# Twelve modulation units: where they run, and five of them on TensorE strips

## The chip, the cores and the metric

The kernel runs on one core of a Trainium2 chip, in float32, with the large products split into float32r pieces. The metric is the device time of one execution in microseconds (us). Several executions are timed, and their median counts. A profile, taken of one execution, shows what the engines did: PE is TensorE (PEld its weight loads), DVE is VectorE, ACT is ScalarE, POOL is GpSimd, SP is SyncE, whose queue issues nearly all transfers.

## The reference, cut to what matters

Two transformer blocks run one after the other on 256 tokens of width 2048. The first is an RWKV7 mixer and a convolutional FFN, each with a modulated norm before it and a gated norm behind it. The modulation is a vector of six segments of 2048 numbers, and its product with a matrix of 2048 x 12288 (100 MB) is what the change is about:

```python
mod = jax.nn.silu(c) @ ada_w + ada_b
sh_m, sc_m, g_m, sh_f, sc_f, g_f = jnp.split((mod + ada_table[layer])[:, None, :], N_MOD, axis=-1)
h = _rms(x, norm_mix_pre[layer]) * (1 + sc_m) + sh_m
y, v_first = _rwkv7_mix(h, ...)          # r, k, v, w, a, g projections, scan over time, @ w_o
x = x + g_m * _rms(y, norm_mix_post[layer])
h = _rms(x, norm_ffn_pre[layer]) * (1 + sc_f) + sh_f
f = _conv_ffn(h, ...)
x = x + g_f * _rms(f, norm_ffn_post[layer])
```

Segments 0 and 1 (sh_m, sc_m) are needed at once. Segment 2 (g_m) is needed when the output projection of the mixer is scaled, segments 3 and 4 (sh_f, sc_f) when the FFN's input is made, segment 5 (g_f) at the FFN's end. The second block (attention, short convolution, gate) takes no part in the change.

## The kernel before

**Stages.** On the profile's clock: a v and k stage to about 300 us; an r stage to about 503 us, a loop over 16 pairs of heads, j, with the projection of r and what the scan needs of each pair; the scan, with a head of its own to about 585 us and then four chunks of 64 tokens to about 745 us; the output projection, four column blocks of w_o, to about 863 us; the residual with its norms and the transposition for the FFN (`add_residual`, `to_fm`) to about 890 us; then the FFN and the second block.

**The head of the scan** is a list of names, HEAD, whose entries are issued in that order: `d` the 32 x 32 diagonal products (`diag_gram`, line 655 on TensorE), `v0` the inversion of the diagonal blocks of half 0 on VectorE (lines 659 to 685), `g` the gram products (line 701), `b` the products with the centring matrix (line 715), `i0` the off-diagonal part of the inversion (lines 735 and 743), `e` one of four e_proj units: one load of w_proj, four matmuls (line 871) and two stores (line 874). The chunk loop behind it issues stage_r (line 757), stage_u (line 774) and the state and output products (from line 788) of a chunk, and beside them, step by step, the inversion of half 1, the norm of the chunk before and the late units.

**The order.** The code's order is not the engines' order. A scheduler reorders instructions under the dependences, and buffers and PSUM banks are taken from pools of fixed size. Within an engine the order is then fixed: an instruction that waits holds those behind it. The SP queue, too, works in order, and a load waits there until its buffer is free.

**Modulation units.** A unit is 512 columns of one segment: 16 row blocks of 128 x 512, loaded two at a time (512 KB a load) into buffers "raw". A unit is cut into four steps of two loads. There are two ways to sum it:

- `ada_group` multiplies each row block by its entries of silu(c) and adds it up, elementwise: VectorE does three of four blocks (lines 240 and 246), ScalarE the fourth (lines 238 and 243) with GpSimd adding (line 244). The 128 rows of the sum are added at the unit's end by matmuls with a column of ones (`ada_fm`, line 281, after line 279 has joined the two sums).
- `ada_group_pe` lets TensorE do the products: the row block is the moving operand, and the stationary one is `sil32`, silu(c) padded with zeros to 32 columns. Four such matmuls stand on four strips of 32 columns of the array and write four quarters of the rows of one PSUM bank ("a"). ScalarE copies the bank at the end (line 268), and `ada_fm` closes the unit as before. Segments 0 and 1 are summed so, in the v and k stage (line 264, loads of line 258).

Twelve late units, segment 2 (units 0 to 3), 4 (units 4 to 7) and 3 (units 8 to 11), go by `ada_group`: 48 steps. A step is taken wherever the code says `next(ada)`: 12 in the r stage (all j but those with j % 8 in RSKIP), 26 in the chunk loop (ASTEP), 6 in the output projection (OSTEP), and the last four where `to_fm` needs the segment. The units of segment 5 have an iterator of their own in the FFN. From the scan on the raw buffers are a ring of three (NADA2), which e_proj shares, against five (NADA) in the v and k stage. Of the PSUM banks with tag "m", used for `ada_fm` and for most short products, the flag `wide_m` makes a third one out of bank "a" when that is not used otherwise.

## Time and profile before

| what | value |
| --- | --- |
| runs timed | 2203.95, 2208.15, 2225.73 us, median 2208.15 |
| the profiled execution, its time | 2202.33 us |
| its span, first to last instruction | 2200.5 us |
| mean granted TensorE clock | 0.938 |
| PE busy | 2007.2 us (91%) |
| DVE busy | 1390.0 us (63%) |
| ACT busy | 1025.5 us (47%) |
| POOL busy | 770.4 us (35%) |
| moved by DMA | 445.26 MB, 202 GB/s in the mean |
| ada_w loads | 192 of 512 KB |
| line 246 (DVE products of the units) | 176, 184.5 us |
| line 244 (POOL sums of the units) | 48, 75.5 us |

Busy shares are means over stages that differ; what matters for a change is the stage it stands in, and in that stage the engine or transfer that the others wait for. The granted clock is a share of 2.4 GHz: 1.0 is the upper level, 0.5 the lower one (1.2 GHz), and a value between is a mix of both. A row of a time order gives the start, the duration, the engine, the line, what is written and read, and how many instructions the row sums up; the bracket at its end is the idle time before it and what ended that.

### The profile page before, as it was taken

The numbers are of one execution on the slowest core, as the hardware profiler recorded it, in microseconds if no ns is written. First come the engines' busy times: TensorE is split into PE (matmuls) and PEld (weight loads), VectorE is DVE, ScalarE is ACT, GpSimd is POOL, SyncE is SP. The second block draws the span as 40 slices with busy tenths as digits, with TensorE's granted clock in tenths as the row PEclk, the third lists the DMA queues.
The fourth block names the chain that finished last, engine by engine and source line by source line (L and its number), as shares of the span: only waits on it lengthen the run. The fifth ranks groups of instructions, "written<-read, shape, count | busy, mean of one in ns | idle before, by whom it ended". The sixth has DMA issues, their size and how long they took to land.

```text
span 2200.5 us, 36863 instructions
## 1 busy us (share of the span) xinstructions
PE 2007.2 (91%) x14708; PEld 1752.7 (80%) x14708; DVE 1390.0 (63%) x1975; ACT 1025.5 (47%) x1594; POOL 770.4 (35%) x437
## 2 busy tenths in 40 slices
PE   6889988987799696899999999999998999999998
PEld 3578777876577475789989999878886799998887
DVE  3576998987877767786666675433335565656435
ACT  3434455553344434555545545444435454454443
POOL 2332445656145334343333232222322222222232
PEclk9999998999679698899999999999999999999999
DMA  8778567774566687676676565665554444456554
GB/s 293 252 249 301 180 207 240 241 230 96 140 160 182 224 288 261 219 270 197 197 215 203 193 209 191 196 214 189 188 190 145 147 158 163 160 163 209 186 194 152
DMA packets 189037, 445.26 MB, mean 202 GB/s; under 512 B 40121, under 2 KB 62777, under 8 KB 187329
## 3 DMA queue, kind: packets, MB, share of 16 engines
q1 hardware_dynamic: 188864, 442.91, 62.4%
q8 instruction: 115, 1.88, 0.3%
q14 instruction: 58, 0.47, 0.1%
HBM read 427.10 MB, written 15.75 MB: 201 GB/s over the span
## 4 chain that ended last, share of the span: by engine, by line
PE 51%; DVE 5%; DMA 4%; ACT 1%; issue 1%; POOL 1%; SPq 0%; ACTq 0%; POOLq 0%; DVEq 0%
PE ps_s L158 6%; PE ps_s L160 6%; PE ps_s L159 5%; PE ps_s L175 4%; PE ps_s L174 4%; PE ps_s L173 4%; PE ps_g L158 4%; PE ps_g L160 4%; PE ps_g L159 4%; PE ps_g L173 3%; PE ps_g L175 3%; PE ps_g L174 3%; DMA raw<-in_ada_w 2%; DVE acc L246 1%; DVE wlo L147 1%
## 5 line engine op out<-in xcount | busy, mean ns | idle before, releaser
L143 ACT ACTIVATE whi<-raw 128x1024 fp32r<-128x1024 f32 x558 | 588.5, 1057 | 647.7 <-PE ps_s L174 126.5
L147 POOL TENSOR_TENSOR wlo<-raw,whi 128x1024 fp32r<-128x1024 f32 x185 | 458.1, 2477 | 984.6 <-ACT whi L143 950.0
L147 DVE TENSOR_TENSOR wlo<-raw,whi 128x1024 fp32r<-128x1024 f32 x373 | 480.3, 1290 | 439.5 <-ACT whi L143 435.2
L160 PE MATMUL ps_g<-xh,wlo 128*128 128x256 f32 x816 | 235.5, 289 | 7.6 <-DVE wlo L147 7.0
L160 PE MATMUL ps_s<-xh,wlo 128*128 128x256 f32 x816 | 230.7, 283 | 9.6 <-DVE wlo L147 9.3
L159 PE MATMUL ps_g<-xl,whi 128*128 128x256 f32 x816 | 235.0, 288 | 2.5 <-POOL xl L1022 2.5
L158 PE MATMUL ps_g<-xh,whi 128*128 128x256 f32 x816 | 235.8, 289 | 0.7 <-DVE kac L407 0.6
L158 PE MATMUL ps_s<-xh,whi 128*128 128x256 f32 x816 | 230.1, 282 | 2.6 <-ACT whi L143 2.6
L159 PE MATMUL ps_s<-xl,whi 128*128 128x256 f32 x816 | 229.6, 281 | 0.0
L246 DVE SCALAR_TENSOR_TENSOR acc<-raw,sil,acc 128x512 f32<-128x512 f32 x176 | 184.5, 1048 | 28.0 <-DMA raw<-in_ada_w 26.6
L160 PEld LDWEIGHTS ps_g<-xh,wlo 128*128 128x128 f32 x816 | 160.5, 197 | 10.4 <-DVE wlo L147 9.6
L160 PEld LDWEIGHTS ps_s<-xh,wlo 128*128 128x128 f32 x816 | 156.5, 192 | 11.4 <-DVE wlo L147 10.7
L159 PEld LDWEIGHTS ps_g<-xl,whi 128*128 128x128 f32 x816 | 161.7, 198 | 4.7 <-POOL xl L1022 2.7
L158 PEld LDWEIGHTS ps_g<-xh,whi 128*128 128x128 f32 x816 | 160.9, 197 | 4.4 <-ACT whi L143 1.3
L158 PEld LDWEIGHTS ps_s<-xh,whi 128*128 128x128 f32 x816 | 156.7, 192 | 3.0 <-ACT whi L143 3.0
L159 PEld LDWEIGHTS ps_s<-xl,whi 128*128 128x128 f32 x816 | 157.3, 193 | 0.0
L244 POOL TENSOR_TENSOR acc<-acc,nbr 128x512 f32<-128x512 f32 x48 | 75.5, 1572 | 140.6 <-ACT nbr L243 139.7
L158 PE MATMUL ps_s<-h3h,whi 128*128 128x256 f32 x384 | 109.6, 285 | 0.0
L160 PE MATMUL ps_s<-h3h,wlo 128*128 128x256 f32 x384 | 108.8, 283 | 0.0
L159 PE MATMUL ps_s<-h3l,whi 128*128 128x256 f32 x384 | 108.4, 282 | 0.0
L373 DVE SCALAR_TENSOR_TENSOR mt<-xx,vec,h 128x256 f32<-128x256 f32 x96 | 75.5, 828 | 6.9 <-POOL yl L377 4.7
L158 PEld LDWEIGHTS ps_s<-h3h,whi 128*128 128x128 f32 x384 | 72.5, 189 | 3.6 <-issue 3.5
(519 smaller groups left out, 4981.7 us busy)
## 6 DMA issues: line engine op xcount, KB each, us to landing
raw<-in_w_f SPq DMA_DIRECT2D x258, 512.0 KB, 4.4
raw<-in_ada_w SPq DMA_DIRECT2D x192, 512.0 KB, 5.2
raw<-in_w_i2f SPq DMA_DIRECT2D x80, 512.0 KB, 3.7
raw<-in_w_o SPq DMA_DIRECT2D x60, 512.0 KB, 4.7
raw<-in_w_v SPq DMA_DIRECT2D x32, 512.0 KB, 4.0
raw<-in_w_k SPq DMA_DIRECT2D x32, 512.0 KB, 4.3
raw<-in_w_r SPq DMA_DIRECT2D x32, 512.0 KB, 6.7
raw<-in_w_g SPq DMA_DIRECT2D x32, 512.0 KB, 4.7
```

Source lines behind the costliest of these rows:

```text
L143: S.activation(hi, raw, AF.Copy)
L147: e.tensor_sub(lo, raw, hi)
L158: mm(acc, wh[:, sl], xh[:, kt, :], start=(kt == 0), stop=False)
L159: mm(acc, wh[:, sl], xl[:, kt, :], start=False, stop=False)
L160: mm(acc, wl[:, sl], xh[:, kt, :], start=False, stop=(kt == KT - 1))
L173: mm(a, xh, wh[:, sl], start=st, stop=False)
L174: mm(a, xl, wh[:, sl], start=False, stop=False)
L175: mm(a, xh, wl[:, sl], start=False, stop=sp_)
L244: G.tensor_tensor(acc, acc, tp, op=ALU.add)
L246: V.scalar_tensor_tensor(acc, raw[:, a, :], sc, acc, op0=ALU.mult, op1=ALU.add)
L373: V.scalar_tensor_tensor(mt[:, i, :], xx[:, k0 + i, :], vcol(V_MU, m * 16 + k0 + i), hx[:, k0 + i, :], op0=ALU.mult, op1=ALU.add)
```

## The change

Three things are changed. **Where the steps are taken:** the r stage takes 4 steps (the last four j in the code, RSTEP) instead of 12, which is all of unit 0; the list HEAD gets 20 entries "a" of one step each, which are units 1 to 5; the 24 steps left, units 6 to 11, are taken in the chunk loop, whose table ASTEP is as before; the output projection takes none, and whatever were left is drained before it. **How five units are summed:** ON_PE names the units 1 to 5, which now go by `ada_group_pe`. **What that needs:** the pool that held `sil32` is closed by then, so `pad_sil` makes it again in the scan's pool, by a memset of GpSimd and a copy of VectorE; and `wide_m` is off during the head, since bank "a" is the accumulator there.

```diff
 NADA2 = 3
-HEAD = "d0 e v0 g0 b0 d1 g1 b1 e i0 e".split()
+HEAD = "d0 e v0 a a a g0 a a a b0 a a a d1 a a a g1 a a a b1 a a a e i0 a a e".split()
 ASTEP = (A01, A01, (0, 1, 1, 0, 1, 1, 0, 1, 1, 0, 1, 1), (1, 1, 1, 1, 1, 1, 0, 0))
-OSTEP = (2, 2, 2, 0)
+OSTEP = (0, 0, 0, 0)
 TFP = 8
-RSKIP = (0, 4)
+RSTEP = 4
+
+ON_PE = (1, 2, 3, 4, 5)
...
-                mm(acc[r:r + 32, :w_], sil32[:, b, :], raw[:, a, :], start=(b < 4), stop=(b >= KT - 4))
+                mm(acc[r:r + 32, :w_], sil32[0][:, b, :], raw[:, a, :], start=(b < 4), stop=(b >= KT - 4))
...
-    sil32 = t_(pa, [P, KT, 32], "sil32")
-    G.memset(sil32, 0.0)
-    V.tensor_copy(sil32[:, :, 0], sil)
+    sil32 = [None]
+
+    def pad_sil(pl):
+        sil32[0] = t_(pl, [P, KT, 32], "sil32")
+        G.memset(sil32[0], 0.0)
+        V.tensor_copy(sil32[0][:, :, 0], sil)
+
+    pad_sil(pa)
...
-    ada_how[0] = ada_group
-    ada = ada_run(ADALAG, *[ada_row(2, k0, 4, V_NMP, gmd) for k0 in range(0, KT, 4)],
-                  *[ada_scale(4, k0, 4, D_AF, V_NFP) for k0 in range(0, KT, 4)],
-                  *[ada_shift(3, k0, 4, D_BF) for k0 in range(0, KT, 4)])
+    late = []
+    for u in range(12):
+        ada_how[0] = ada_group_pe if u in ON_PE else ada_group
+        k0 = u % 4 * 4
+        late.append(ada_row(2, k0, 4, V_NMP, gmd) if u < 4 else ada_scale(4, k0, 4, D_AF, V_NFP) if u < 8
+                    else ada_shift(3, k0, 4, D_BF))
+    ada = ada_run(ADALAG, *late)
...
-        if j % 8 not in RSKIP:
+        if j >= NPAIR - RSTEP:
             next(ada, None)
...
     pc_ = phs.enter_context(pool("scan", 1, reuse_waits="tile"))
+    pad_sil(pc_)
+    wide_m[0] = False
...
     for nm in HEAD:
         run(HD[nm]())
     ada_pool[0] = 1
+    wide_m[0] = True
...
+    for _ in ada:
+        pass
     ada_pool[0] = 1
     phb.close()
```

Line numbers of the changed kernel are higher: by 2 up to the stages, by 10 to 15 behind them (655 is 667, 735 is 747, 788 is 800, 264 is 266, 246 is 248, 228 is 230).

On TensorE, ahead of the first state product of chunk 0 (line 788), these rows stand in the kernel before; `TQ` is the inverted diagonal block, `raw` with `ys` an e_proj unit, `uv` and `rs` are operands of the first chunk:

```order
2440 L743 MATMUL ps_m<-xh,TQ 32x32 x32
2441 L871 MATMUL ps_g<-raw,ys 128x512 x3
2442 L757 MATMUL ps_s<-uv,xh 64x64 x8
2443 L735 MATMUL ps_a<-TQ,xl 32x32 x16
2444 L735 MATMUL ps_m<-TQ,xl 32x32 x16
2445 L757 MATMUL ps_s<-uv,xh 64x64 x8
2446 L774 MATMUL ps_s<-rs,xh 64x64 x8
2447 L757 MATMUL ps_s<-uv,xh 64x64
2448 L743 MATMUL ps_m<-xl,TQ 32x32 x16
2449 L743 MATMUL ps_a<-xl,TQ 32x32 x16
2450 L757 MATMUL ps_s<-uv,xh 64x64 x7
2451 L788 MATMUL ps_g<-uv,BK 64x64 x2
```

In the changed kernel the same place, ahead of line 800, reads as follows; `raw` with `sil` are the units (the buffer's name is sil32, its digits are cut off):

```order
2461 L266 MATMUL ps_a<-raw,sil_4959 32x512 x2
2462 L769 MATMUL ps_s<-uv,xh 64x64 x3
2463 L786 MATMUL ps_s<-rs,xh 64x64 x16
2464 L266 MATMUL ps_a<-raw,sil_4959 32x512 x4
2465 L283 MATMUL ps_m<-cst,nbr 128x1 x4
2466 L747 MATMUL ps_m<-TQ,xl 32x32 x16
2467 L266 MATMUL ps_a<-raw,sil_4959 32x512 x8
2468 L883 MATMUL ps_g<-raw,ys 128x512 x4
2469 L266 MATMUL ps_a<-raw,sil_4959 32x512 x8
2470 L883 MATMUL ps_g<-raw,ys 128x512 x4
2471 L747 MATMUL ps_a<-TQ,xl 32x32 x16
2472 L800 MATMUL ps_g<-uv,BK 64x64 x2
```

Between the stage_r and stage_u products and the first state product stand now the end of unit 4, all 16 matmul pairs of unit 5 and two e_proj units.

On the SP queue, the head of the scan begins in the kernel before with these rows (`ed` are stores of e_proj, `gmd` one of a finished segment-2 unit, `bl` and `gl` loads of the first chunk's norm):

```order
190 L694 DMA uv<-vd 64x2048 x2
191 L874 DMA ed<-gl 128x512 x2
192 L826 DMA bl<-bd 128x16x64
193 L228 DMA raw<-in_ada_w 128x2x512
194 L826 DMA bl<-bd 128x16x64
195 L228 DMA raw<-in_ada_w 128x2x512
196 L922 DMA NT<-in_w_o 128x1024
197 L874 DMA ed<-gl 128x512
198 L228 DMA raw<-in_ada_w 128x2x512
199 L874 DMA ed<-gl 128x512
```

and in the changed kernel with these:

```order
190 L706 DMA uv<-vd 64x2048
191 L260 DMA raw<-in_ada_w 128x2x512
192 L886 DMA ed<-gl 128x512
193 L260 DMA raw<-in_ada_w 128x2x512
194 L886 DMA ed<-gl 128x512
195 L260 DMA raw<-in_ada_w 128x2x512 x2
196 L316 DMA gmd<-adav 128x4x1
197 L260 DMA raw<-in_ada_w 128x2x512 x8
198 L316 DMA gmd<-adav 128x4x1
199 L260 DMA raw<-in_ada_w 128x2x512 x8
200 L316 DMA gmd<-adav 128x4x1
```

The rows shown hold 20 ada loads where those of before hold three. Two loads of unit 1 and one of w_proj are issued in the r stage already; the other 38 loads of units 1 to 5 and two more of w_proj then stand in this queue, and all of them belong to matmuls ahead of the first state product.

On VectorE, the residual stretch before (line 983 is the residual, line 1002 the scaling for `to_fm`, line 246 a unit's product):

```order
866 L983 SCALAR_TENSOR_TENSOR xt<-y_8004,rsy,xt 128x512 x2
867 L1051 TENSOR_TENSOR y_8004<-ps_s,grow 128x512
868 L983 SCALAR_TENSOR_TENSOR xt<-y_8004,rsy,xt 128x512 x2
869 L246 SCALAR_TENSOR_TENSOR acc_8644<-raw,sil,acc_8644 128x512
870 L975 TENSOR_REDUCE rsy<-ssq 128x1
871 L246 SCALAR_TENSOR_TENSOR acc_8644<-raw,sil,acc_8644 128x512 x2
872 L338 RECIPROCAL rsy<-rsy 128x1
873 L246 SCALAR_TENSOR_TENSOR acc_8644<-raw,sil,acc_8644 128x512
874 L983 SCALAR_TENSOR_TENSOR xt<-y_8004,rsy,xt 128x512 x4
875 L975 TENSOR_REDUCE rsx<-ssq_8553 128x1
876 L246 SCALAR_TENSOR_TENSOR acc_8644<-raw,sil,acc_8644 128x512
877 L338 RECIPROCAL rsx<-rsx 128x1
```

and in the changed kernel (lines 998, 1017 and 248):

```order
839 L998 SCALAR_TENSOR_TENSOR xt<-y_8105,rsy,xt 128x512 x3
840 L1066 TENSOR_TENSOR y_8105<-ps_s,grow 128x512
841 L998 SCALAR_TENSOR_TENSOR xt<-y_8105,rsy,xt 128x512
842 L248 SCALAR_TENSOR_TENSOR acc_10496<-raw,sil,acc_10496 128x512
843 L990 TENSOR_REDUCE rsy<-ssq 128x1
844 L248 SCALAR_TENSOR_TENSOR acc_10496<-raw,sil,acc_10496 128x512
845 L340 RECIPROCAL rsy<-rsy 128x1
846 L998 SCALAR_TENSOR_TENSOR xt<-y_8105,rsy,xt 128x512 x4
847 L990 TENSOR_REDUCE rsx<-ssq_8580 128x1
848 L340 RECIPROCAL rsx<-rsx 128x1
849 L1017 TENSOR_SCALAR y_8105<-xt,rsx 128x512 x4
```

Between the rows of the residual five products of a unit stood; now there are two, and these belong to segment 5: the scheduler has moved the first steps of the FFN's units forward, and eleven of their loads stand among those of w_o on the SP queue, beside the last eight of the late units.

## Rows read from the trace of the kernel before

**Rows 1.** Table by stage; us, busy us of PE, PEld, DVE, ACT, POOL, clock, DMA.

```profile
core 0: us, PE busy (x) PEld busy (x) DVE busy (x) ACT busy (x) POOL busy (x), PEclk, DMA share, GB/s
300.00:503.00 203.00, 179.08 (x1207) 158.76 (x1206) 178.03 (x241) 115.83 (x222) 117.92 (x109) 0.92 0.70 221
505.00:585.00 80.00, 54.74 (x952) 42.10 (x942) 67.84 (x173) 28.34 (x58) 37.12 (x22) 0.77 0.46 117
585.00:745.00 160.00, 144.54 (x1931) 116.66 (x1930) 117.61 (x233) 76.22 (x169) 69.17 (x55) 0.78 0.66 176
745.00:863.00 118.00, 100.00 (x399) 77.49 (x398) 81.95 (x91) 45.08 (x62) 47.71 (x23) 0.87 0.78 272
863.00:890.00 27.00, 7.25 (x32) 5.44 (x30) 24.91 (x35) 14.01 (x33) 11.52 (x6) 0.60 0.79 271
890.00:980.00 90.00, 80.98 (x644) 78.58 (x643) 71.16 (x86) 46.37 (x69) 37.95 (x19) 0.95 0.72 241
```

**Rows 2.** The same table for four shorter stretches.

```profile
20.00:30.00 10.00, 5.79 (x49) 2.34 (x44) 6.75 (x12) 1.64 (x4) 0.00 (x0) 0.78 1.04 371
...
425.00:434.00 9.00, 9.00 (x70) 8.37 (x69) 7.98 (x13) 5.26 (x12) 6.48 (x7) 1.00 0.57 186
...
540.00:560.00 20.00, 7.93 (x50) 5.08 (x49) 20.00 (x39) 6.22 (x13) 13.85 (x12) 0.78 0.09 26
560.00:580.00 20.00, 16.01 (x180) 10.77 (x181) 19.74 (x39) 6.39 (x13) 1.81 (x1) 0.54 0.44 141
```

**Rows 3.** Instructions of line 607, one per j of the r stage.

```profile
L607 DVE TENSOR_TENSOR AR<-ps_g,ep x16: 407/413/426, 340.8 to 502.6; 128x256 f32<-128x256 f32 x16
```

**Rows 4.** Lines of VectorE, 341 to 503 us; count, busy us, mean ns, idle before.

```profile
L246 DVE SCALAR_TENSOR_TENSOR acc<-raw,sil,acc 128x512 f32<-128x512 f32 x33 | 37.5, 1138 | 0.9 <-DMA raw<-in_ada_w 0.8
```

**Rows 5.** Waits, 341 to 503 us: us in total, times, longest.

```profile
ACT whi L143 <- DMA raw<-in_w_r: 19.4, 7, 5.0
```

**Rows 6.** Ada loads: issue to landing, 500 to 585 us, and the whole program.

```profile
DMA to landing us min/median/max: 3.7/3.7/3.8
...
raw<-in_ada_w SPq DMA_DIRECT2D x192, 512.0 KB, 5.2
```

**Rows 7.** TensorE in time order, v stage: start, us, line; one ada step.

```profile
38.17 1.07 PE L264 MATMUL ps_a<-raw,sil 128*32 128x512 f32 x8
```

**Rows 8.** The SP queue in time order: start, us, count of loads.

```profile
47.82 7.18 SPq L258 DMA_DIRECT2D raw<-in_ada_w  x4
...
523.28 2.04 SPq L874 DMA_DIRECT2D ed<-gl  x2
...
703.99 12.27 SPq L228 DMA_DIRECT2D raw<-in_ada_w  x4
```

**Rows 9.** TensorE in time order, head; in brackets idle and releaser.

```profile
501.90 0.38 PE L655 MATMUL ps_s<-AR,BK 64*32 64x32 f32 x12
...
516.86 0.58 PE L701 MATMUL ps_m<-AR,BK 64*128 64x128 f32 x1
...
528.23 1.23 PE L715 MATMUL ps_m<-cst,BK 128*128 128x128 f32 x8
...
563.99 1.88 PE L735 MATMUL ps_m<-TQ,xh 32*32 32x32 f32 x32 [15.91 <-DVE TQ L725]
...
585.26 0.27 PE L788 MATMUL ps_g<-uv,BK 128*64 128x64 f32 x1
```

**Rows 10.** Chain that ended last, 863 to 891 us, and 740 to 905 us.

```profile
by line: DVE xt L983 32.3%; DVE acc L246 19.7%; DVE y L1002 19.1%; PE ps_m L1006 8.9%; issue 6.7%; DVE y L1051 4.3%; PE ps_a L1006 3.8%; DVE rsy L338 1.2%; ACT rsy L337 1.0%; ACT whi L143 0.9%; ACT junk L970 0.9%; PE ps_g L158 0.8%; PE ps_s
...
821.05 11.05 DMA raw<-in_ada_w
...
881.54 4.06 DVE y L1002 x2
...
885.67 0.79 DVE y L1002 x2
```

**Rows 11.** Lines of VectorE, 890 to 980 us.

```profile
L246 DVE SCALAR_TENSOR_TENSOR acc<-raw,sil,acc 128x512 f32<-128x512 f32 x22 | 26.7, 1216 | 1.2 <-DMA raw<-in_ada_w 0.9
```

## The prediction

> **What bounds the kernel now.** I read the stage table first, then inside each stage the waits, the grouped lines and the time order of the engine that the change touches. The span is 2200.5 us of a profiled execution of 2202.33 us; the runs shown have their median at 2208.15, 0.26% above it, and their lowest at 2203.95. TensorE is busy for 91% of the span, so a gain can only come from the stretches in which it is not: of the 678 us from the r stage to the first part of the FFN it is busy 566.6 us [rows 1], and 111 us are left to win. They lie as follows: 24 us in the r stage, 25 in the head of the scan, 15 in the scan, 18 in the output projection, 20 in the residual stretch and 9 in the first 90 us of the FFN [rows 1]. All twelve late units lie in these stages. They cost VectorE, ScalarE, GpSimd and the SP queue, and nothing on TensorE but the few matmuls that close a unit.
>
> **The r stage loses 8 of its 12 steps.** One product of VectorE comes per j, from 340.8 to 502.6 us over 15 intervals, so a j takes 10.79 us [rows 3]. VectorE and TensorE are both near full there (178.0 and 179.1 us of 203) [rows 1]. A load is 128 x 1024 and holds two row blocks of 512; a step has two loads, hence four products of 512 columns, three on VectorE and one on ScalarE and GpSimd. Eight steps are then 16 loads and 24 VectorE products of 1.138 us [rows 4], together 27.3 us, or 1.7 us per j. Above, the gain is bounded by the fastest j in the trace, 9.00 us with TensorE busy for all of it at a granted clock of 1.00 [rows 2]: 15 x (10.79 - 9.0) = 27 us. Below it is 0, if the loads of w_r are the limit: ScalarE waits 19.4 us for them in this stage [rows 5]. But the ada loads stand in the same queue, and 16 of 24 of them go, so this wait falls too. I take a little over half, 15 us (9.8 us per j).
>
> **The head gains 20 steps, all of them units 1 to 5, summed on TensorE.** Their cost on TensorE is small. One step of two loads is 1.07 us of it in the v stage [rows 7], so 20 steps are 21 us, and ahead of the second inversion product TensorE waits 15.91 us for VectorE [rows 9]; in 540 to 560 us it is busy 7.9 us of 20 and the DMA engines for 9% [rows 2]. The cost on VectorE falls, since no late product stands there any more. What decides is the loads. In the new order of TensorE all five units stand ahead of the first state product of chunk 0, with two e_proj units, so 40 loads of 512 KB go through a ring of three buffers before the scan proper can start; before, that product comes at 585.26 us, 83.4 us behind the head's start, its first diagonal product at 501.90 us [rows 9]. The ring starts to turn when e_proj has freed its buffer and its outputs are stored, at 525.3 us now [rows 8], 23.4 us behind the start. With p us per load and 4 us for the last landing the product comes 27.4 + 40p us behind the start.
>
> - p = 1.8 is the rate of the same kind of units in the v stage, where the queue spends 7.18 us on four loads with five buffers [rows 8]: 99.4 us, which is 16 us later than before. Of that I take back 4 us, a fifth of the 20 us from 560 to 580 us, of which VectorE is busy for 19.7 [rows 2]: it is rid of the late products there, and more products of stage_r and stage_u of chunk 0 then stand ahead of that state product. So **+12 us**.
> - Lower bound: p = 1.41, a load at the 371 GB/s that 20 to 30 us reach [rows 2]: 83.8 us, or -4 us after the same 4 us.
> - Upper bound: a buffer is held for the landing, 5.2 us in the median [rows 6], and about 1.4 us more (0.5 us of matmuls, and an estimate for their turn on TensorE), and three in flight give p = 2.2: 115.4 us, so +28 us.
>
> The trace nearest to the new head is its own emptiness: loads landed in 3.7 us there, against 5.2 in the whole program [rows 6]; (3.7 + 0.5)/3 is 1.4, so 1.8 leaves a margin for the fixed order of TensorE. The Trainium skill, "DMA: Bandwidth & Descriptors", Anatomy of one DMA, gives about 2.0 us fixed per DMA plus the bytes at 436 GB/s. That would be an estimated 3.2 us per load, and with the matmuls about 1.2 us for each of three buffers; a head term could not be lower than the -4 us of the bandwidth. The trace's 3.7 us is slower and is what the sum goes by.
>
> The POOL memset and the VectorE copy that pad the vector again stand at the scan's start, and so does the loss of the third "m" bank. The first are one instruction each and lie beside the diagonal products of TensorE: 0. For the bank no row gives a price: 0 if the two "m" banks and the copies keep pace, else a part of the gram products' 11.4 us from 516.86 to 528.23 us [rows 9]; I take 0, since TensorE waits for VectorE right behind them anyway.
>
> **The scan** has 24 steps instead of 26, with their loads in nearly the same rows of SP: 0.
>
> **The output projection** sheds its own six steps, but the scheduler pulls eleven loads of the FFN's seg-5 units into the places: 19 ada loads stand among w_o where some 24 stood. One stall there, of 11.05 us, is on the chain for an ada load [rows 10]. It needs the queue to be less crowded by more than a fifth to go; I take 4 us, between 0 and 11.
>
> **The residual stretch** (863 to 890 us) is VectorE's: it is busy 24.9 of 27 us [rows 1]. 19.7% of the chain of 28 us are late products, 5.5 us [rows 10]. Between the rows of the residual five of them stood, and two are left. The scaling on line 1002 takes 4.06 us for two and 0.79 us for the next two [rows 10], so some of it is stretched by what runs beside it. I take 7 us, from 4 (the products alone) to 11 (with all that is stretched).
>
> **The FFN's first part** loses about 17 of the 22 products that fill 26.7 us of VectorE [rows 11]; TensorE's idle there is 9 us. I take 5, between 0 and 9.
>
> **Sum.** -15 + 12 + 0 - 4 - 7 - 5 = -19 us, which makes 2183 us against the profiled execution. The runs lie up to 0.26% above that, and I forecast **2185 us**.
>
> **Rivals.**
>
> *Nothing to measure.* The r stage stays at its pace since TensorE is at a clock of 0.92 and w_r's loads are late, so that it gives 5 us, and the seg-5 steps that are pulled forward fill what is freed, so that the rest gives 7: -12 + 12 = 0, **2202 us**. For it: VectorE waits only little for anything in r, and TensorE is as full as it. Against it: the fastest j.
>
> *Slower.* One mechanism: TensorE takes its rows in order, all five units share one accumulator bank and three buffers, and each matmul of a unit that waits for its load holds the inversion and state products behind it. The scan's queue shows the pace if buffers are freed by busy engines: 12.27 us for four loads, p = 3.07 [rows 8]. The product then comes 27.4 + 122.8 = 150 us behind the start, +63 us after the 4 us, and with -31 elsewhere the time is **2234 us**. It decides from p = 2.3 upward, where the head eats the 31 us. Beside it the clock: after its wait of 15.91 us TensorE runs at a granted 0.54 in 560 to 580 us [rows 2, 9], nearly all of it at the lower level. If the units' matmuls come spread between waits, they run at that level too, and their 21 us become up to 42: 2185 + 21 = 2206 us, still within 1% of the kernel before, and so part of the case above. The Trainium skill, "TensorE: Matmul & The Clock Gate", HAM oscillation, describes this for kernels whose matmuls wait for a DMA between short bursts: the array falls to the low clock each time. The trace agrees as far as that stretch goes. Against the slower case: the DMA engines have little else to do in the head.
>
> *More gain.* The r stage falls to 9.0 us per j and loads flow at p = 1.41: -27 - 4 - 4 - 7 - 5 = -47, **2155 us**. For it: the DMA engines are at 9% in 540 to 560 us.
>
> **How the numbers follow.** The forecast's case has 0.54, nothing 0.17, slower 0.15, more gain 0.14. A kernel like this tells about 1% from no change, so the borders are 2186 and 2230 us. The forecast's own range, 2168 to 2202 us, lies on both sides of the first: 0.31 of it is faster, 0.23 the same. Faster by over 1%: 0.31 + 0.14 = 0.45; within 1%: 0.23 + 0.17 = 0.40; slower: 0.15. The range goes from 2153 us, which takes in the case of more gain, to 2220 us, a head at p = 2.2 (+28) with only 10 us won elsewhere; what lies outside is the slow case and a little on each end.
>
> **What would show it.** In the trace of the changed kernel: the VectorE product of line 607 (now 617) every 9.8 us; the first state product (line 788, now 800) about 96 us behind the head's start; no wait of some 16 us of TensorE at the first inversion product, but matmuls of units 2 and 3 there; four loads of the head in some 7.2 us of the queue; the residual stretch at 20 us. The prediction is wrong if p is over 2.3, if TensorE's clock in the head falls well below 0.77, or if the r stage stays above 10.5 us per j.

## The result, and the profile after

The changed kernel takes 2228.48 us in the median (2221.09 to 2240.42), the kernel before beside it 2208.66 us (2195.51 to 2225.73). The ratio is 1.0086, 95% interval 1.006 to 1.0113: about 0.9%, or 20 us, slower. That is inside the 1% that was called "no change", but above the forecast of 2185 us and above the end of its range, 2220 us.

The profiled execution of the changed kernel took 2237.74 us (span 2235.8 us), a long one among its runs, and that of before 2202.33 us, a short one. The two traces therefore differ by 35 us where the medians differ by 20. Stages can be compared by what they win and lose, but a difference of a few us in one stage of one execution is not to be read. The stage table of the changed kernel (stretch, its length, busy us with instruction counts of PE, PEld, DVE, ACT and POOL, granted clock, DMA share, GB/s) answers to [rows 1]:

```profile
core 0: us, PE busy (x) PEld busy (x) DVE busy (x) ACT busy (x) POOL busy (x), PEclk, DMA share, GB/s
345.00:488.00 143.00, 134.91 (x983) 124.28 (x981) 109.93 (x169) 83.69 (x166) 84.65 (x91) 0.97 0.66 208
487.90:648.10 160.20, 127.92 (x1221) 64.02 (x1220) 73.38 (x240) 33.33 (x67) 39.65 (x21) 0.73 0.63 160
648.10:864.30 216.20, 183.92 (x2067) 144.93 (x2066) 149.69 (x220) 92.00 (x188) 89.68 (x65) 0.77 0.68 204
864.30:923.00 58.70, 58.01 (x254) 47.30 (x253) 38.60 (x35) 26.64 (x36) 23.02 (x11) 1.00 0.90 323
923.00:945.00 22.00, 3.15 (x15) 2.22 (x14) 19.98 (x28) 12.15 (x30) 10.78 (x5) 0.60 0.57 196
945.00:1035.00 90.00, 89.02 (x767) 88.22 (x767) 59.80 (x77) 52.62 (x77) 28.04 (x13) 0.98 0.55 181
```

The second line is the head, from the first diagonal product to the first state product: 160.2 us where it was 83.4 [rows 9]. The r stage, the output projection, the residual and the FFN are shorter, and the scan is longer. By the first and last instructions of the stages, with the stages of before measured in the same way:

| stretch | before us | after us | difference | forecast |
| --- | --- | --- | --- | --- |
| up to the r stage | 340.8 | 345.2 | +4.4 | 0 |
| r stage, first to last AR product, and on to the head | 161.1 | 142.7 | -18.4 | -15 |
| head, to the first state product | 83.4 | 160.2 | +76.8 | +12 |
| scan, to the first product of w_o's result | 205.1 | 216.2 | +11.1 | 0 |
| output projection, to the first sum for the norm | 74.3 | 59.5 | -14.8 | -4 |
| residual, and on to the first FFN result | 53.9 | 41.3 | -12.6 | -7 |
| FFN, first to last result | 492.1 | 484.8 | -7.3 | -5 |
| rest | 785.7 | 781.8 | -3.9 | 0 |

The column adds up to the 35 us between the spans. The head costs 77 us, and everything else together wins 41. The stages here do not end where those of the forecast do: the residual itself, from the first sum for the norm to the start of the last scaling row, went from 23.1 us (864.7 to 887.8) to 20.5 us (923.8 to 944.3), and 10.0 of the 12.6 us lie between that row and the first FFN result.

TensorE in time order in the new head (start, us, line; `x8` is one step with all four row blocks at hand, `x4` one load of two row blocks; in brackets idle time and what ended it):

```profile
496.18 1.07 PE L266 MATMUL ps_a<-raw,sil 128*32 128x512 f32 x8
...
510.74 1.89 PE L266 MATMUL ps_a<-raw,sil 128*32 128x512 f32 x4 [1.29 <-DMA raw<-in_ada_w]
...
519.21 1.05 PE L266 MATMUL ps_a<-raw,sil 128*32 128x512 f32 x4 [0.37 <-DMA raw<-in_ada_w]
...
570.22 1.92 PE L266 MATMUL ps_a<-raw,sil 128*32 128x512 f32 x4 [4.46 <-DMA raw<-in_ada_w]
...
582.81 3.62 PE L747 MATMUL ps_m<-TQ,xh 32*32 32x32 f32 x64
...
648.08 0.34 PE L800 MATMUL ps_g<-uv,BK 128*64 128x64 f32 x4
```

The inversion products of line 747 have no bracket: the 15.91 us for which TensorE waited there for VectorE [rows 9] are gone. In their place stand unit matmuls, nearly all as `x4`, and many behind a wait for a load. An `x4` row takes 1.05 us, or 1.89 to 1.92 us, where `x8` takes 1.07. So a load that is summed alone costs TensorE as much as two loads together, and the 20 steps take 56.6 us instead of the 21 us of the forecast. By groups of lines and by waits in the head (count, busy us, mean ns, idle before; then us in total, times, longest):

```profile
L266 PE MATMUL ps_a<-raw,sil 128*32 128x512 f32 x160 | 56.6, 866 | 26.0 <-DMA raw<-in_ada_w 26.0
```

```profile
PE ps_a L266 <- DMA raw<-in_ada_w: 26.0, 14, 4.8
```

The SP queue in the head, to compare with [rows 8] (start, us, count):

```profile
506.95 21.73 SPq L260 DMA_DIRECT2D raw<-in_ada_w  x8
528.74 0.56 SPq L316 DMA_DIRECT2D gmd<-adav  x1
529.38 26.71 SPq L260 DMA_DIRECT2D raw<-in_ada_w  x8
...
563.76 32.94 SPq L260 DMA_DIRECT2D raw<-in_ada_w  x6
596.75 0.46 SPq L316 DMA_DIRECT2D gmd<-adav  x1
599.45 21.53 SPq L260 DMA_DIRECT2D raw<-in_ada_w  x6
```

The 38 loads of line 260 issued in the head run from 497.27 to 633.99 us, 3.6 us each. Their landings (least, median, most) and those of the four small stores of a finished gate unit:

```profile
DMA to landing us min/median/max: 3.5/5.3/11.6
```

```profile
gmd<-adav SPq DMA_DIRECT2D x4, 2.0 KB, 9.5
```

### The profile page after: what moved, and what is told of

It is laid out like the page before. It is cut to its first block, busy times and chain, and to the rows that moved or that the text cites. A ratio compares the mean times of both kernels' runs of the same rounds, so it can differ in the third digit from the quotient of the medians.

```text
span 2235.8 us, 37165 instructions
## 1 busy us (share of the span) xinstructions
PE 2057.6 (92%) x14868; PEld 1755.7 (79%) x14868; DVE 1316.1 (59%) x1916; ACT 1017.9 (46%) x1579; POOL 735.1 (33%) x418
## 4 chain that ended last, share of the span: by engine, by line
PE 64%; DMA 7%; DVE 6%; ACT 2%; issue 2%; POOL 1%; SPq 0%; ACTq 0%; DVEq 0%; POOLq 0%
PE ps_s L160 6%; PE ps_s L162 6%; PE ps_s L161 6%; DMA raw<-in_ada_w 5%; PE ps_g L162 5%; PE ps_g L160 5%; PE ps_g L161 5%; PE ps_g L177 4%; PE ps_g L175 4%; PE ps_s L175 4%; PE ps_s L177 4%; PE ps_s L176 4%; PE ps_g L176 4%; PE ps_a L266 2%; DVE acc L248 2%
## 5 line engine op out<-in xcount | busy, mean ns | idle before, releaser
L161 PEld LDWEIGHTS ps_g<-xl,whi 128*128 128x128 f32 x816 | 157.0, 192 | 1.5 <-POOL xl L1037 0.9
L248 DVE SCALAR_TENSOR_TENSOR acc<-raw,sil,acc 128x512 f32<-128x512 f32 x121 | 121.7, 1006 | 39.4 <-DMA raw<-in_ada_w 38.3
L266 PE MATMUL ps_a<-raw,sil 128*32 128x512 f32 (+1 forms) x480 | 98.7, 652 | 33.6 <-DMA raw<-in_ada_w 33.4
L246 POOL TENSOR_TENSOR acc<-acc,nbr 128x512 f32<-128x512 f32 x33 | 50.7, 1535 | 188.5 <-ACT nbr L245 185.7
```

Of the source, the lines that this page charges most:

```text
L161: mm(acc, wh[:, sl], xl[:, kt, :], start=False, stop=False)
L246: G.tensor_tensor(acc, acc, tp, op=ALU.add)
L248: V.scalar_tensor_tensor(acc, raw[:, a, :], sc, acc, op0=ALU.mult, op1=ALU.add)
L266: mm(acc[r:r + 32, :w_], sil32[0][:, b, :], raw[:, a, :], start=(b < 4), stop=(b >= KT - 4))
```

## The experiments

The tables below give the head from the first diagonal product to the first state product, as read from the profiled execution of each run: first its length, then the part up to the first inversion product, TensorE's busy time and granted clock in it, the busy time of the unit matmuls and their wait for loads, all in us; last the ratio of the whole time to the kernel before.

### What a step costs in the head: none, 8, 12, 20

```diff
# e4_nohead: head as before, the 44 steps in the chunk loop
-HEAD = "d0 e v0 a a a g0 a a a b0 a a a d1 a a a g1 a a a b1 a a a e i0 a a e".split()
+HEAD = "d0 e v0 g0 b0 d1 g1 b1 e i0 e".split()
+ASTEP = ((1,) * 12, (1,) * 12, (1,) * 12, (1,) * 8)
+ON_PE = ()
-    pad_sil(pc_)
-    wide_m[0] = False
# v_head8 (and v_head12, with four steps more): the r stage keeps its 12 steps
+HEAD = "d0 e v0 a a g0 b0 d1 g1 b1 a a a a a a e i0 e".split()
+ON_PE = (3, 4)
+        if j % 8 not in (0, 4):
# v_r12h20: 12 steps in r, 20 in the head, 16 in the scan
+ASTEP = ((0, 0, 1) * 4, (0, 0, 1) * 4, (0, 0, 1) * 4, (0, 1, 0, 1, 0, 1, 0, 1))
+ON_PE = (3, 4, 5, 6, 7)
```

The last three, like e1_noscatter below, have no gate units in the head. e4_nohead differs from the others in one thing more: since nothing is summed in bank "a", the third "m" bank stays in use, and no padded vector is made.

> The r stage and the output projection as in the changed kernel, the head as before it; the other 44 steps are spread over the chunk loop (VectorE). It takes the head's part of the change away. If the gains read from the two traces (r stage 20 us, output projection and residual 17, first FFN part 20) belong to the moves alone they stay here: first state product about 20 us earlier than in the kernel before. The scan has 20 more steps, 60 VectorE products of about 1 us and 40 loads: 30 to 60 us longer where these are on the path, so the whole 2170 to 2205. If the gains were a product of the long head, they vanish here.

> The r stage as in the kernel before (12 steps, units 0 to 2, segment 4); two units (8 steps) on TensorE in the head, without small stores, behind the gram products of both halves; 28 steps in the chunk loop; none in the output projection. Theory: 16 loads at 2.4 us lie behind the 44 to 60 us of VectorE's inversion, so the head is 78 to 90 us, r is 162 us as before, the scan 205 to 215 us, and the output projection to first FFN block is shorter by 25 to 35 us than before. Sum 2175 to 2195. Rival: the head's loads come on top as in the changed kernel (2.9 us per step) and the scan's two extra steps cost 4 us each: 2195 to 2210.

> As the run with two units in the head, but three (12 steps), and 24 steps in the chunk loop, where the changed kernel has them as well. Theory: 24 loads at 2.4 us take 58 us and reach just beyond the inversion, so the head is 90 to 100 us, the scan some 8 us shorter than with 28 steps; 2175 to 2195. Rival: each step in the head costs 2.9 us from the first on: head 110 us, 2200 to 2210.

> The r stage with 12 steps as in the kernel before, the head with 20 steps (units 3 to 7, segments 4 and 3, without the small stores), the chunk loop with 16 steps, the output projection with none. Against the run with 4, 20 and 24 steps the r stage gets 20 us back (2.5 us per step), and the scan and its tail lose 8 steps at about 4 us: 32 us less. Expected 2200 to 2210, against 2219 and 2213 for the kernel before. If a step costs the same wherever it stands (2.5 to 3 us), it stays at 2215 to 2222.

| run | head | to inversion | PE busy | clock | units | wait | ratio, interval |
| --- | --- | --- | --- | --- | --- | --- | --- |
| before | 83.4 | 62.1 | 56.9 | 0.77 | none | none | 1 |
| after | 160.2 | 94.9 | 127.9 | 0.73 | 56.6 | 26.0 | 1.0086, 1.006 to 1.0113 |
| e4_nohead | 75.1 | 52.2 | 59.0 | 0.76 | none | none | 1.0179, 1.0124 to 1.0235 |
| v_head8 | 100.8 | 62.2 | 81.9 | 0.76 | 21.9 | 0.6 | 1.0045, 1.0013 to 1.0077 |
| v_head12 | 115.9 | 71.3 | 96.4 | 0.78 | 31.9 | 15.4 | 1.0086, 1.0055 to 1.0116 |
| v_r12h20 | 126.4 | 76.8 | 108.6 | 0.89 | 46.1 | 9.3 | 1.0032, 1.001 to 1.0054 |

The head grows from the first step on: 8 steps cost 26 us against e4_nohead, 12 cost 41, 20 cost 51. That is the price of the steps together with that of the third bank. It does not show that the head has no slack: in v_head8 TensorE still waits 13.4 us in front of the first inversion product, and 24 of its 64 unit matmuls stand behind that wait. There the inverse was written by 556.7 us and TensorE went on at 565.69, just after VectorE had copied a finished unit's sum out of an "m" bank, at 565.38. That some 9 us of the wait were for the bank is argued from these times, not shown; the profile names another row of VectorE.

Elsewhere a step has a price, too: in the r stage 19.9 us for 8 (2.5 each), behind the scan some 35 us for 10 (3.5 each), and in the chunk loop, where e4_nohead has 44 of them, the stretch from the first state product to the first product of w_o's result takes 302.1 us against 216.2 with 24 (4.3 each). By the stage table the 20 steps in the head may cost (18.4 + 34.7 - 11.1)/20 = 2.1 us each before the gains elsewhere are eaten, beyond the 83.4 us of the head before. The changed kernel is at 3.8, v_r12h20 at 2.2, though its other stages have other steps, so the border holds for it only roughly.

Every time in this group came out above what was expected for it. v_head8 and v_head12 took 2224 and 2234 us, where 2175 to 2195 was expected and 2195 to 2210 by the rivals; e4_nohead took 2251, where 2170 to 2205 was expected; v_r12h20 took 2223, next to the 2215 to 2222 of a step that costs the same wherever it stands.

### What of it are the loads, and what the small stores

```diff
# e1_noscatter: segments 4 and 3 first, the gate units (segment 2) in the scan
-        k0 = u % 4 * 4
+        seg, k0 = ((4, 0), (4, 4), (4, 8), (4, 12), (3, 0), (3, 4), (2, 0), (2, 4), (2, 8), (2, 12), (3, 8), (3, 12))[u]
# e8_noload: the same, and only the first load of each late unit
+            if seg < 2 or q == 0:
+                raw = t_(adap[0], [P, 1024], "raw").rearrange("p (a c) -> p a c", c=w_)
```

> The changed kernel with the twelve units in another order: segments 4 and 3 fill the r stage and the head, the four units of segment 2 stand in the scan, so no store of 512 four-byte pieces (gmd, 8.7 to 10.2 us to land) stands among the head's loads. In the changed kernel the head (first diagonal product to first state product) is 160 us. Theory S, the small stores hold up the loads behind them: the four longest load waits of the chain, 7.9, 12.4, 11.6 and 7.7 us, fall to about 5 us, the head to 140 us or less, the whole to about 2205. Theory R, the ring of three buffers with TensorE's fixed order paces the head whatever the stores do: the head stays at 153 us or more, the whole within 8 us of the changed kernel.

> The run without the small stores (head 133 us), but each unit on TensorE loads only its first 512 KB and multiplies it eight times: 35 of the head's 40 unit loads are left out (the output is then not the reference's), all matmuls stay. Theory R, the loads through the ring are what lengthens the head: the head falls to 95 us or less (75 us is the head without any step). Theory T, the matmuls on TensorE do: the head stays at 115 us or more.

Head, and unit matmuls in it, of e8_noload and of e1_noscatter:

```profile
482.30:578.70 96.40, 80.94 (x1219) 49.04 (x1220) 79.57 (x244) 32.22 (x63) 32.53 (x21) 0.90 0.39 107
```

```profile
L267 PE MATMUL ps_a<-raw,sil 128*32 128x512 f32 x160 | 26.5, 625 | 0.3 <-ACT nbr L271 0.3
```

```profile
484.80:618.00 133.20, 111.93 (x1219) 59.07 (x1218) 75.72 (x240) 33.24 (x67) 40.78 (x21) 0.85 0.66 193
```

```profile
L266 PE MATMUL ps_a<-raw,sil 128*32 128x512 f32 x160 | 45.1, 713 | 13.5 <-DMA raw<-in_ada_w 13.5
```

So the 85 us between a head without steps (75.1) and that of the changed kernel (160.2) fall into three parts, if the profiled executions are taken at their word:

- Without loads the head takes 96.4 us: +21.3 us for 20 steps, just above the 95 us up to which the loads alone were to be the cause. TensorE is busy 21.9 us longer than in e4_nohead (80.9 and 59.0 us), which is the price of [rows 7] and the 21 us of the forecast. Its idle time is the same, 15.5 and 16.1 us, but it is another wait. In e4_nohead TensorE waits 11.9 us for the inverse (first row below). In e8_noload the steps fill that wait, and two rows of gram and centring products wait 13.1 us until VectorE has copied a finished unit's sum out of the "m" bank that they are to write (line 286); VectorE comes to that copy in the middle of its inversion. The head has two "m" banks here and three in e4_nohead. Whether a third would close this wait was not tried.

```profile
PE ps_a L745 <- DVE TQ L735: 11.9, 1, 11.9
```

```profile
528.33 2.07 PE L714 MATMUL ps_m<-AR,BK 64*128 64x128 f32 x14 [4.14 <-DVE adav L286]
...
549.60 1.11 PE L728 MATMUL ps_m<-cst,BK 128*128 128x128 f32 x4 [8.95 <-DVE adav L286]
```

- With the loads of e1_noscatter 133.2 us: +36.8. The unit matmuls take 45.1 us instead of 26.5, since loads are summed alone or at the low clock, TensorE waits 13.5 us for loads, and its other rows take longer.
- With the stores of the gate units 160.2 us: +27.0. Such a store is 2 KB in 512 pieces of 4 bytes. The head of the changed kernel has some 2,100 more small packets than that of e1_noscatter, in which the loads land in 4.1 us in the median and 7.1 at most, against 5.3 and 11.6. Two more pairs of runs differ in the same way: e2_strips4 and e7_both (head 154.8 and 130.2 us, median landing 5.5 and 4.7), e11_ring5stores and e10_ring5 (145.9 and 131.9 us, median landing 9.3 and 4.5). What differs in each pair is the units that stand in the head, so the few other rows that close a gate unit go with its stores. The whole times do not follow as clearly: the first two pairs are 0.5% and 0.4% apart, and the pair with five buffers, at 1.0008 and 1.004 with intervals that overlap, shows no gain from it. The two DMA lines are those of the changed kernel and of e1_noscatter:

```profile
DMA packets 18497, 25.69 MB, mean 160 GB/s; under 512 B 7056, under 2 KB 7312, under 8 KB 18356
```

```profile
DMA packets 16381, 25.68 MB, mean 193 GB/s; under 512 B 4944, under 2 KB 5200, under 8 KB 16240
```

One execution of e8_noload took 2164.2 us, 51 us less than the median of the kernel before, where 19 us were forecast: without 35 of the head's 40 loads the change would win more than it was to win. e1_noscatter gave 2219.3 us, ratio 1.0038 (1.0011 to 1.0065). It wins a little over half of the loss back, some 11 us, less than the 27 us of its head.

### The ways out: buffers, strips, order

```diff
# e6_ring2: two buffers in place of three
+NADA2 = 2
# e10_ring5 (with e1_noscatter) and e11_ring5stores (with the stores): two "bl" tiles of the scan as buffers 4 and 5
+            if adaph[0] is not None and k >= NADA2:
+                raw = t_(adaph[0], [P, NPAIR, 64], "bl", bufs=NGL).rearrange("p a b -> p (a b)")
# e2_strips4, and e7_both (with e1_noscatter): a load is four row blocks of 256 columns
+            qa, h, hn, hw = (q % 4, q // 4, 4, 256) if seg > 1 else (q, 0, n, w_)
# e9_smallmm (with e1_noscatter): row blocks 5 to 16 only 32 columns wide
+                wm = w_ if seg < 2 or b < 4 else 32
# e5_early (with e1_noscatter), and v_ring5early (with e10_ring5): both halves' gram products ahead of the steps
+HEAD = "d0 e v0 a a a g0 b0 d1 g1 b1 a a a a a a a a a a a a a a a e i0 a a e".split()
# e3_dvehead: the head's units elementwise, as before
+ON_PE = ()
```

> The changed kernel with two raw buffers instead of three from the r stage on. In the changed kernel 40 loads take 160 us of head, 4.0 us each. Theory R, each buffer is held for landing and turn, so the pace goes as one over the number of buffers: 5.5 to 6 us per load, head 215 us or more. If loads are not the limit (theory T or O) the head grows by less than 20 us.

> The run without the small stores (head 133 us, three buffers) with five buffers for the head's unit loads: two tiles of the scan that stand idle until its first norm (bl) join the ring. Theory R, three buffers let the loads run ahead by three only, so that their time adds to TensorE's other rows in place of lying beside them: the head falls to 105 to 118 us, towards the 96 us without loads, the wait for loads from 13.5 us (TensorE) to under 6, the whole by 15 to 25 us to about 2195 to 2205. If the loads' own rate is the limit (512 KB at the DMA engines' pace), the head stays at 127 us or more.

> The changed kernel, small stores and all (head 160 us), with five buffers for the head's unit loads as in the run above. Theory R and S are separate: the stores still delay what is behind them, but five buffers cover part of a delay; head 125 to 140 us. If the stores' harm is full, the head stays above 150 us.

> The changed kernel, but a load of a strip unit holds four row blocks of 256 columns (1 KB pieces) in place of two of 512, so each load uses all four strips. In the changed kernel the 160 matmuls of the units take 56.6 us of TensorE in the head, where 21 were expected. Theory T, TensorE's price (two strips at a time, half of them at the lower clock) is what lengthens the head: the matmuls fall to about 30 us, the head from 160 to 130 us, the whole by 30 us. Theory R, the loads pace it: matmul time falls, the wait for loads grows by as much, the head stays within 10 us of 160.

> No small stores in the head (segments 4 and 3 there) and loads of four row blocks by 256 columns, so that each load uses all four strips: the two edits of earlier runs together. The first alone gave a head of 133 us, the second alone 155, the changed kernel has 160. Theory T, with loads that land in 4 us TensorE's price is what is left: matmuls 45 to some 27 us, head 115 us or less. Theory R, the loads' pace through three buffers is left: head 127 us or more.

> The run without the small stores (head 133 us), all loads kept, but the last twelve of a unit's sixteen row blocks are multiplied in 32 columns of 512 only (the output is then not the reference's): the matmuls fall from 45 us to about 15. Theory T: the head falls by 25 us or more, to 108 us. Theory R: the wait for loads takes the place of the matmuls, the head falls by less than 10 us.

> The run without the small stores, with the list HEAD in another order: the diagonal, gram and centring products of both halves stand ahead of all steps from the fourth on, so that on TensorE they no longer stand between the loads' matmuls. Same 20 steps, same loads. In the run without the small stores the first inversion product comes 76 us and the first state product 133 us behind the first diagonal product; VectorE's inverse is ready at 43.5 us. Theory O, TensorE's fixed order of gram and unit products costs the 32 us between inverse and product: the first inversion product comes at 55 us or less, the first state product at 110 to 118 us. Theory R, forty loads through three buffers set the end whatever stands between: the inversion product may come earlier, the state product stays within 6 us of 133.

> Five buffers, no small stores, and the diagonal, gram and centring products of both halves ahead of the steps from the fourth on. With three buffers that order was 9 us longer than the other (142 to 133 us), since three loads stood full while TensorE did its other rows. With five the loads run on in that time: head 100 to 115 us, the whole 2190 to 2205. If the order itself is bad, it stays 9 us behind the run with five buffers in the other order.

> The changed kernel with the head's 20 steps in the same places of the code, but summed on VectorE, ScalarE and GpSimd (no unit on TensorE). Theory O, the fixed order of TensorE (matmuls that wait for loads hold the inversion and state products) makes the head long: the first state product comes back to 85 to 100 us behind the first diagonal product, the time goes into the scan, whose loads and VectorE products grow, the whole 2190 to 2215. Theory R, forty loads through three buffers take their time whoever sums them and the scheduler keeps them ahead of the scan: head still 130 us or more, the whole 2220 or more.

| run | head | to inversion | PE busy | clock | units | wait | ratio, interval, or us of one execution |
| --- | --- | --- | --- | --- | --- | --- | --- |
| e6_ring2 | 199.3 | 129 | 131.6 | 0.70 | 58.3 | 59.2 | 2302.44 us |
| e11_ring5stores | 145.9 | 94 | 119.8 | 0.74 | 50.4 | 20.0 | 1.0008, 0.9977 to 1.004 |
| e1_noscatter | 133.2 | 75.9 | 111.9 | 0.85 | 45.1 | 13.5 | 1.0038, 1.0011 to 1.0065 |
| e10_ring5 | 131.9 | 78 | 115.4 | 0.78 | 47.2 | 7.4 | 1.004, 1.0012 to 1.0068 |
| e2_strips4 | 154.8 | 96 | 109.6 | 0.69 | 34.5 | 36.4 | 1.0069, 1.0043 to 1.0095 |
| e7_both | 130.2 | 76 | 104.9 | 0.74 | 33.1 | 13.6 | 1.0025, 1.0006 to 1.0045 |
| e9_smallmm | 137.7 | 77 | 105.9 | 0.65 | 21.8 | 22.2 | 2223.79 us |
| e5_early | 141.8 | 84 | 118.0 | 0.82 | 51.8 | 15.7 | 0.9996, 0.9966 to 1.0026 |
| v_ring5early | 131.8 | 78 | 113.4 | 0.75 | 49.9 | 12.6 | 1.0025, 1.0006 to 1.0044 |
| e3_dvehead | 182.8 | 119 | 82.9 | 0.60 | none | none | 1.0245, 1.0193 to 1.0297 |

- **Depth.** Two buffers instead of three cost 39 us of head and, in one execution, 74 us of the whole; five instead of three win 14 us with the small stores and 1 us without. So far as these traces tell, three are short where some loads land late.
- **Less matmul time.** The unit matmuls fall from the 45 us of e1_noscatter to 33 in e7_both and to 22 in e9_smallmm. The head stays at 130 and 138 us. What falls is the granted clock, 0.85 to 0.74 and 0.65. In e9_smallmm the rows of TensorE that are not units take 84 us (105.9 - 21.8) where they took 67 in e1_noscatter (111.9 - 45.1).
- **Earlier independent work.** e5_early puts the gram products of both halves ahead; the head gets longer in its trace (141.8 us to the 133.2 of e1_noscatter), though its ratio is not higher (0.9996 and 1.0038, intervals that overlap). That the head is long because TensorE's program order holds these products behind late loads falls with it, and with v_ring5early (131.8 us to the 131.9 of e10_ring5).
- **Units on VectorE.** Worse by 23 us of head, and by 1.6% of the whole than the changed kernel: to sum them on TensorE was right.

Lengths and ratios do not go together below about 1%: e11_ring5stores and e5_early have longer heads than e10_ring5 and lower ratios. The head is that of one execution, and the ratio that of four to fourteen, on several chips.

### Two limits at once, and the first inversion product

Still open was why no single relief helped. v_ring5s4 gives three: no small stores, five buffers, four strips a load. v_i0 changes the order of TensorE's rows, too, so that the first inversion products stand behind two units; v_i0r3 has that order with the loads and buffers of e1_noscatter.

```diff
# v_i0, v_i0r3
+HEAD = "d0 e v0 a a a g0 b0 a a a a a i0 d1 g1 b1 a a a a a a a a a a a a e e".split()
```

> The changed kernel with three edits at once: no gate units in the head (so none of the stores of 4-byte pieces, as in e1_noscatter), five load buffers (as in e10_ring5), and loads of four row blocks by 256 columns, so that the four strips of a step are at hand together (as in e2_strips4). The order of TensorE's rows is that of the changed kernel. If two limits lie close together (loads at 3 to 4 us a step, TensorE's rows at a low clock), relieving both at once shortens the head, where each alone did not: the first diagonal product to the first state product in 105 to 118 us (e1_noscatter 133.2, e10_ring5 131.9, e7_both 130.2), the unit matmuls busy below 38 us, and the kernel at 0.990 to 0.998 of the time before. If the head is instead held by the order of rows on TensorE alone (products and sums of the steps queued ahead of the inversion), 126 to 134 us again, the part from the first inversion product to the first state product above 50 us, and 1.000 to 1.005.

> As v_ring5s4, and TensorE's program order in the head is changed: the first half's inversion products stand right behind two units of steps, ahead of the second half's gram products, so that VectorE's second inversion is not queued in front of what they need. If the row order costs the 24 us by which the stretch from the first diagonal product to the first inversion product grew (52 us without steps, 76 with them), that stretch is 50 to 60 us here, and the head 10 to 25 us shorter than in v_ring5s4, unless the second half then ends as late: the second inversion on VectorE starts behind the gram products, now some 15 to 20 us later, and takes about 45 us, in which case the state products start as before but stall in the second half, and the time stays within 0.3% of v_ring5s4. If the row order is worth nothing, the first stretch stays at 74 us or more.

> The row order of v_i0 with the loads and the three buffers of e1_noscatter (no gate units in the head, two row blocks by 512 columns a load). It tells the row order's worth by itself: against e1_noscatter (head 133.2 us, of it 76 to the first inversion product, 1.0038 of the time before). Row order the cause of part of the head: first stretch 50 to 62 us, the kernel 0.993 to 1.001. The loads and TensorE's busy time alone the cause: first stretch shorter but the scan longer by as much, 1.001 to 1.006.

| run | head | to inversion | PE busy | clock | units | wait | ratio, interval |
| --- | --- | --- | --- | --- | --- | --- | --- |
| v_ring5s4 | 124.5 | 78.5 | 102.8 | 0.75 | 31.2 | 5.9 | 1.0009, 0.9985 to 1.0034 |
| v_i0 | 122.2 | 43.2 | 102.0 | 0.78 | 33.6 | 9.3 | 0.9988, 0.9957 to 1.0019 |
| v_i0r3 | 126.9 | 41.0 | 106.3 | 0.88 | 45.6 | 15.8 | 1.002, 0.9995 to 1.0044 |

v_ring5s4 comes out between its two expectations, 124.5 us, where one said 105 to 118 and the other 126 to 134: relief of both limits is worth some 6 to 9 us of head, not 20. In v_i0 the first inversion product comes 43 us behind the start, even sooner than in a head without steps (52.2), but the first state product gains only 2 us. In v_i0r3, too, the first part shrinks from 76 to 41 us and the head by 6 us only; its ratio of 1.002 is that of the reading by which the scan's start gains nothing. In the time order of TensorE in v_i0 the old wait for VectorE is back, too:

```profile
529.61 3.59 PE L758 MATMUL ps_m<-TQ,xh 32*32 32x32 f32 x64 [6.14 <-DVE TQ L748]
```

```profile
486.40:529.60 43.20, 31.44 (x715) 22.00 (x715) 37.07 (x120) 10.45 (x20) 23.70 (x12) 0.96 0.82 231
529.60:608.60 79.00, 70.51 (x730) 45.62 (x730) 40.23 (x121) 24.74 (x51) 10.26 (x9) 0.68 0.63 194
```

What TensorE did not do in the first 43 us it does in the 79 behind, busy for 70.5 of them at a granted clock of 0.68. So the 24 us by which the first part had grown (52 us without steps, 76 with them) were no loss by themselves, and the row order is not the main cause. What all heads with 20 steps, their loads and no small stores have in common is that TensorE is busy for 102 to 118 us ahead of the first state product, at a mixed clock, and idle for 17 to 32 us in waits of one kind or another; without loads it is idle for 15.5 us as well. In v_ring5s4 the longest of these waits is for a bank, as in e8_noload:

```profile
PE ps_m L724 <- DVE adav L295: 8.4, 1, 8.4
```

Such waits take 1.3 us in e1_noscatter, 4.2 in e10_ring5, 8.4 in v_ring5s4 and 13.1 in e8_noload, and the waits for loads 13.5, 7.4, 5.9 and none. So part of what shorter waits for loads set free goes into waits for the two "m" banks. In v_i0 there is none of them, and the wait for the inverse is back instead. How far a third bank would shorten the head stays open, since no run has the 20 steps and that bank.

By the sum above v_ring5s4 stands at (124.5 - 83.4)/20 = 2.05 us a step and v_i0 at 1.94, about where the gains are used up, and their ratios are 1.0009 and 0.9988. None of the versions that do all the work is measurably faster than the kernel before; e5_early, e11_ring5stores, v_ring5s4, v_i0 and v_i0r3 cannot be told from it.

## Why the prediction was wrong

**The r stage** was right in its direction and a little small: AR products every 9.46 us (141.9 us over 15 intervals) where 9.8 was forecast and the fastest j allowed 9.0.

```profile
L617 DVE TENSOR_TENSOR AR<-ps_g,ep x16: 409/424/426, 345.2 to 487.1; 128x256 f32<-128x256 f32 x16
```

**The output projection, the residual and the FFN** were right in direction and together too small, 35 us where 16 was forecast. The residual itself, put at 7 us, gave 2.6 in these two traces, below its lower bound of 4; what made the sum too small is the output projection (14.8 for 4) and the 10 us that were won between the scaling and the first FFN result. In the output projection TensorE is now busy for 58.0 of 58.7 us; the stall for an ada load was one of several that went. In the residual stretch the late products fall from 19.7% of the chain [rows 10] to 6.3%:

```profile
by line: DVE xt L998 58.9%; ACT junk L985 10.4%; DVE acc L248 6.3%; issue 4.3%; PE ps_m L1021 4.2%; ACT whi L145 2.9%; DVE y L1066 2.7%; ACT rsx L339 2.7%; ACT tf L1034 2.6%; DVE y L1017 2.3%; ACT rsy L339 1.3%; DVE rsy L340 1.2%; DVE rsx L
```

**The scan** was put at 0 and lost 11 us in the trace. VectorE has as many products of the units there as before, 72, so the steps are not more. TensorE is busy for 183.9 us instead of 176.7 at the same clock. What it is was not tried.

**The head is the step that failed**, +77 where +12 was forecast, and it failed in both of its terms, the time per load and the overlap of TensorE's rows; a third, the bank, was put at 0 and is not 0.

The first was p, the time per load. It was put at 1.8 us from the v stage [rows 8], with 2.2 as the upper bound. It is 3.6 in the changed kernel and 2.9 in e1_noscatter (38 loads in some 111 us). The bound took the median landing of the whole program and 1.4 us for the matmuls' turn, (5.2 + 1.4)/3. The landing was right, 5.3 us. The turn was not: 3 x 3.6 - 5.3 leaves 5.5 us in which a buffer waits for TensorE. The rate of the v stage came from five buffers and from a TensorE that was busy there, too, 19.4 us of the 22 from 38 to 60 us, but at a granted clock of 1.00. The fixed part of the formula, 27.4 us, was near for no good reason: the first of the 38 loads is issued 9.4 us behind the head's start, not 23.4, and the state product comes 14.1 us behind the last, not 4.

The rival "slower" had the nearest price, 3.07 from the scan's own queue [rows 8], and gave 2234 us. Its mechanism, rows of TensorE in order behind late loads through three buffers, is half of it: the waits for loads are there, 26.0 us, but other orders of the rows brought the state product sooner by only 2 and 6 us (v_i0, v_i0r3) or not at all (e5_early). It was given 0.15, for the reason that "the DMA engines have little else to do in the head". They had four small stores to do, which the SP rows shown ahead of the prediction contained, and without which the head of e1_noscatter is 27 us shorter.

The second was TensorE's own price. It was said to be 21 us, hidden behind a wait of 15.91 us [rows 9] (which stands in front of the first inversion product, not the second). With loads the unit matmuls take 56.6 us. Without them, in e8_noload, TensorE is busy 21.9 us longer than without steps, as forecast, and the old wait is filled, but the head is still 21.3 us longer, since waits of 13.1 us for the banks came in its place. That is the third term: of the lost "m" bank the prediction said that no row gave a price, and took 0, since TensorE waits for VectorE right behind those products anyway. In the changed kernel itself TensorE waits for loads first, and no wait of its rows for a bank shows.

The wait of before is a wait for VectorE's inversion of half 0, and when TensorE gets to those products later, because steps stand in front of them, VectorE has long gone on to half 1: its inverse was written from 532.3 us on, and TensorE took it up at 582.8. A wait in front of one row is room only for work that is there in time and that ends in time, and here it is followed by a part in which TensorE is the bound. The table by part shows what became of VectorE, first up to the inversion product and then from there to the first state product, in the changed kernel:

```profile
487.90:582.80 94.90, 76.20 (x811) 39.78 (x810) 70.49 (x236) 17.98 (x33) 39.65 (x21) 0.78 0.66 162
582.80:648.10 65.30, 51.71 (x411) 24.24 (x410) 2.89 (x5) 15.35 (x34) 0.00 (x0) 0.66 0.58 159
```

In the 65 us of the second part VectorE is busy for 2.9 and GpSimd not at all. Before, VectorE was busy for nearly all of the stretch from 560 to 580 us [rows 2]. From the bound beside TensorE it has become an engine that waits for TensorE, and so the products and the copies that the change took from it are no gain in the head.

The clock belongs to the second term. The prediction named 0.77 as the border; the head has 0.73, its second part 0.66, and the unit matmuls show both levels, 1.05 and 1.92 us. The Trainium skill, "TensorE: Matmul & The Clock Gate", HAM oscillation, describes kernels whose short bursts of matmuls wait for a DMA and fall to the low clock each time. The trace agrees in part: rows of 1.9 us stand behind waits for loads here, as at 570.22 us, and in e9_smallmm, with even shorter bursts, the clock fell to 0.65; but the row at 519.21 us, behind a wait of 0.37 us, took 1.05 us, and between 586 and 599 us unit rows of 1.92 us stand among the products of lines 755 and 769 with no wait for a load. The doubling to 42 us that the prediction mentioned as a mishap came out larger, 56.6 us, since single loads came on top.

Of the signs named in advance, the r stage and the missing wait of 16 us came as said, and the residual stretch was put at 20 us for 27 and is 20.5 by the rows named above, which had taken 23.1 before. The first state product 96 us behind the head's start came 160 us behind it; four loads in 7.2 us took 11 to 22 us; the two conditions "p over 2.3" and "clock below 0.77" both came true.

## What to carry to other kernels

Work that an engine takes in program order ahead of the row that everything else waits for is to be priced with its loads at the pace of that place (here 2.9 to 3.6 us a load), not at that of another stage with more buffers, and a wait seen in front of one row is not room for it until one can say which row would end earlier. A bank or buffer that is given up has a price, too: ask which engine frees those that are left, and what stands in front of that on the engine (here 13.1 us, where 0 was put). Before moving transfers into a stretch that looks empty, list every transfer that goes with them; four stores of 2 KB in 4-byte pieces went with 14 to 27 us of head. When relief of one limit leaves the time where it was, relieve two at once before believing in a third.

## What the runs showed of the hardware that was not expected

- A column strip that works alone or in a pair saves no time: two row blocks of 512 columns take 1.05 us on two strips, four take 1.07 us on four; in e8_noload one block on one strip takes 1.05 us, too. The Trainium skill, "TensorE: Matmul & The Clock Gate", Measured speedup vs the span model, puts the time of a pack at that of one matmul and about 4 ns for each further tile; the two rows agree with it.
- Four stores of 2 KB in 4-byte pieces took 8.7 to 10.2 us to land, where a load of 512 KB takes 3.5 us at best. With them in the queue the median landing of the loads rose from 4.1 to 5.3 us, and the longest from 7.1 to 11.6 us; with five buffers the median rose from 4.5 to 9.3 us.
- Fewer columns for TensorE did not shorten the stretch: in one execution with the unit matmuls at half their time the granted clock fell from 0.85 to 0.65, and the other rows took 84 us instead of 67.
